# A hybrid decoder trunk on one core: the buffers of the two rings of split weights begin 64 bytes further each

## The chip, the cores and the metric

The kernel runs on 1 core of one Trainium2 chip. Its time is the device time of one execution in microseconds; three executions of the kernel before gave 1941.78, 1944.04 and 1953.4, the median being 1944.04 us.

## The reference

Two layers of a decoder trunk over one sequence of 256 tokens, 1024 channels wide, all in float32. Per layer:

```python
mod = silu(c) @ w_ada[l] + b_ada[l]            # shifts, scales, gates
h = x * (1 + sc1) + sh1
proj = h @ w_in[l]                             # feeds four mixers
y = einsum('bsnc,ncd->bsnd', four_mixers(proj), w_br[l])
mix = (sigmoid(gates) * y).sum(branches) @ w_out[l]
x = layer_norm(alpha * x + g1 * mix)
h = x * (1 + sc2) + sh2
f = swiglu(h)            # layer 0: dense, 2816 wide
f = moe_swiglu(h)        # layer 1: 8 experts of 3584, 2 per token
x = layer_norm(alpha * x + g2 * f)
```

The four mixers are block attention with ALiBi, retention, an SSD scan and stick-breaking attention. Nearly all of the bytes are weights, which are read once.

## The kernel before

Every weight is multiplied as a sum of two parts. A weight tile of 128 partitions by 2048 floats (1 MB) arrives from memory in a tile `raw`. Half of it, 128 by 1024, is then split: ScalarE copies it into a tile `whi` of the type float32r, which keeps its upper bits, and VectorE subtracts that copy from the original and writes the rest into `wlo` (`split_upto`, lines 286 to 310). The activations are split in the same way (hhi and hlo, ohi and olo, ghi and glo, ehi and elo). A product is then three matmuls, high by high, high by low and low by high (`mm3`, lines 380 to 385).

`whi` and `wlo` are two rings of HALVES = 5 tiles, each 4,096 bytes of a partition. `half` (line 339) has the splitting run AHEAD = 3 halves in front of the matmuls that use them. `raw` is a ring of 3 tiles, to which 5 tiles `raw2` come in the second layer's expert part (RAW and RAW2, line 238), so that five of eight places there are raw2. Each `raw` that has been split makes room, and SyncE issues the next transfer in its queue (`emit_dma`, line 240), in an order of weights that is fixed in a list (`build_order`). A few more places for tiles lie in crow, acc, ghi, glo and others that are free at that time (`emit_into`, line 263).

The mixers' projections and the gate and up parts of the dense feed-forward stream the 256 tokens of hhi and hlo through loaded pieces of 128 by 128 of whi and wlo (256 columns each). The experts stream 512 columns of whi or wlo through loaded activations of up to 128 tokens (ghi, glo, ehi, elo).

The pools of tiles lie one behind the other in a partition's memory of 229,376 bytes: constants, `x`, hhi and hlo, the rows (crow and acc among them), then the pool `st` with raw, whi and wlo in the order of their first use, and behind it the tiles of a mixer or of a feed-forward part, which take each other's place. The starts, in bytes of a partition:

| tiles | start | remainder by 512 |
|---|---|---|
| hhi, hlo | 33,216 and 41,408 | 448 |
| crow, acc | 49,600 and 57,792 | 448 |
| raw, 3 of 8,192 | 74,240 | 0 |
| whi, 5 of 4,096 | 98,816 | 0 |
| wlo, 5 of 4,096 | 119,296 | 0 |
| first tile behind the rings | 139,776 | 0 |
| raw2, 5 of 8,192 | 147,968 | 0 |
| ghi, glo, 3 each of 4,096 | 188,928 and 201,216 | 0 |
| ohi, olo, 3 each of 4,096 | 195,232 and 207,520 | 160 |
| end of the highest tile | 228,464 | |

Of the kernel before, what the change touches and what calls it, by code (L numbers as in the profile page):

```python
# [9 lines left out]
F32 = mybir.dt.float32  # L10
F32R = mybir.dt.float32r
# [7 lines left out]
P = 128  # L19
# [125 lines left out]
def trunk(ctx: ExitStack, tc: tile.TileContext, I, out, dbg=None):  # L145
    nc = tc.nc
    pe, act, dve, pool = nc.tensor, nc.scalar, nc.vector, nc.gpsimd
# [6 lines left out]
    st = ctx.enter_context(tc.tile_pool(name="st", bufs=1))  # L154
# [83 lines left out]
    RAW, RAW2, HALVES, AHEAD = 3, 5, 5, 3  # L238
# [34 lines left out]
    def pop_raw(i):  # L273
        raws.pop(i)
        again.pop(i, emit_dma)()

    def raw_upto(i):

        while state["raw"] < i:
            n = state["raw"]  # L280
            if order[n][1] is not None:
                order[n][1](raws[n])
                pop_raw(n)
            state["raw"] += 1

    def split_upto(q):
        while state["half"] <= min(q, 2 * len(hls) - 1):
            q0 = state["half"]
            i, h = hls[q0 // 2], q0 % 2
            raw_upto(i)  # L290
            hi = st.tile([P, 1024], F32R, name="whi", bufs=HALVES)
            lo = st.tile([P, 1024], F32R, name="wlo", bufs=HALVES)
            if isinstance(raws[i], tuple):
                m = len(raws[i]) // 2
                src = raws[i][h * m:(h + 1) * m]
            else:
                n = 512 if q0 in (0, 2 * len(hls) - 1) else 1024
                src = [raws[i][:, c:c + n] for c in range(h * 1024, (h + 1) * 1024, n)]
            n = 1024 // len(src)
            for j, raw in enumerate(src):  # L300
                c = slice(j * n, (j + 1) * n)
                act.activation(hi[:, c], raw, AF.Copy)  # L302
                while later:
                    later.pop()()
                dve.tensor_sub(lo[:, c], raw, hi[:, c].bitcast(F32))  # L305
                late_lo()
            parts[q0] = (hi, lo)
            if h == 1:
                pop_raw(i)
            state["half"] += 1  # L310
# [28 lines left out]
    def half(fs):  # L339

        q = state["done"]
        split_upto(q)
        flush()
        split_upto(q + AHEAD)
        for f in fs(*parts.pop(q)):
            f()
        state["done"] += 1
        step()
        if q - state["mix"] in EXTRA[state["mix"] > 0]:
            step()  # L350

    def by_token(fs, end):

        q = state["done"]
        for i in range(4):
            split_upto(q + i)
            flush()
            split_upto(min(q + i + AHEAD, q + HALVES - 1))
            for f in fs(0, i, *parts[q + i]):
                f()  # L360
            step()
        end(0)
        for i, h in ((0, 1), (0, 2), (1, 1), (1, 2), (2, 1), (3, 1), (2, 2), (3, 2)):
            for f in fs(h, i, *parts[q + i]):
                f()
            if h == 2:
                parts.pop(q + i)
                state["done"] += 1
                step()
            elif i == 3:  # L370
                end(1)
        end(2)
# [88 lines left out]
    def late_lo():  # L461
        while los:
            dve.tensor_sub(*los.pop())
# [1136 lines left out]
```

## Time and profile before

| what | us |
|---|---|
| median of three executions | 1944.04 |
| lowest and highest | 1941.78 and 1953.4 |
| the profiled execution | 1946.45 |
| its span, first to last instruction | 1944.6 |
| TensorE busy | 1884.3 |
| VectorE busy | 1623.0 |
| ScalarE busy | 1200.6 |
| GpSimd busy | 187.8 |

The profile is that of one execution. Matmuls overlap, so their durations add up to more than the time they take; how fast TensorE goes is read from the distance of two starts. The granted clock of TensorE is given as a share of 2.4 GHz. The first layer's mixer lasts to about 380 us, its dense feed-forward to about 565 us, the second layer's mixer to about 940 us, and the experts take the rest.

### The profile page before, as it was taken

Reading aid. Unit: us, or ns where it says so; the run is one execution under the profiler, and the core shown is the slowest. Engines: PE = TensorE matmul, PEld = TensorE weight load, DVE = VectorE, ACT = ScalarE, POOL = GpSimd, SP = SyncE. Lnnn points to the kernel's source line nnn. Section 1 sums busy time; section 2 is a strip of 40 time slices with the busy share of each in tenths; the row PEclk is TensorE's granted clock in tenths of the full one; section 3 lists DMA queues with packets and bytes.
Section 4 is the critical chain, followed back from the end, with each engine's and each line's share of the span. In section 5 each row is a group of like instructions: output and inputs, shape, how many; then the busy total and the mean of one; then the engine's idle time right before and its main releaser. Section 6 shows DMA issues by size and latency. Waiting matters only on the chain. (4 is left out here: it accounts for less than half of the span.)

```text
span 1944.6 us, 29158 instructions
## 1 busy us (share of the span) xinstructions
PE 1884.3 (97%) x11276; PEld 1642.2 (84%) x11276; DVE 1623.0 (83%) x2017; ACT 1200.6 (62%) x1526; POOL 187.8 (10%) x178
## 2 busy tenths in 40 slices
PE   6999999999999999999999999999999999999997
PEld 5888989899989889999888888888888888888885
DVE  7776876888767687767898999999999899999987
ACT  4546544544445456344677777777777777777774
POOL 0023332110011142320000000000000000000000
PEclk9999999999999999999999999999999999999999
DMA  9565666377744456655899899998999999999992
GB/s 346 189 246 212 232 227 228 133 282 290 283 142 174 173 197 232 237 195 218 325 385 329 323 367 366 360 378 323 362 374 360 372 337 350 376 346 378 361 366 105
DMA packets 84340, 558.14 MB, mean 287 GB/s; under 512 B 9697, under 2 KB 9953, under 8 KB 22242
## 3 DMA queue, kind: packets, MB, share of 16 engines
q1 hardware_dynamic: 82226, 550.30, 75.8%
q0 software_dynamic: 1824, 5.78, 0.9%
q8 instruction: 90, 1.47, 0.3%
q14 instruction: 56, 0.46, 0.1%
q10 hardware_dynamic: 144, 0.11, 0.0%
HBM read 555.12 MB, written 1.05 MB: 286 GB/s over the span
## 5 line engine op out<-in xcount | busy, mean ns | idle before, releaser
L305 DVE TENSOR_TENSOR wlo<-raw,whi 128x1024 fp32r<-128x1024 f32 (+1 forms) x880 | 1048.9, 1232 | 202.9 <-ACT whi L302 201.2
L302 ACT ACTIVATE whi<-raw 128x1024 fp32r<-128x1024 f32 (+1 forms) x880 | 881.0, 1050 | 143.2 <-DMA raw<-in_win_dram 29.3
L382 PE MATMUL mm<-hhi,whi 128*128 128x256 f32 x1376 | 393.9, 286 | 19.2 <-ACT whi L302 15.5
L384 PE MATMUL mm<-hhi,wlo 128*128 128x256 f32 x1376 | 387.5, 282 | 8.2 <-DVE wlo L305 8.2
L383 PE MATMUL mm<-hlo,whi 128*128 128x256 f32 x1376 | 387.3, 281 | 0.5 <-DVE hlo L580 0.3
L382 PE MATMUL mm<-whi,ghi 128*128 128x512 f32 x896 | 350.0, 391 | 0.0
L384 PE MATMUL mm<-whi,glo 128*128 128x512 f32 x896 | 349.2, 390 | 0.0
L383 PE MATMUL mm<-wlo,ghi 128*128 128x512 f32 x896 | 348.8, 389 | 0.0
L382 PEld LDWEIGHTS mm<-hhi,whi 128*128 128x128 f32 x1376 | 264.5, 192 | 28.1 <-ACT whi L302 17.6
L384 PEld LDWEIGHTS mm<-hhi,wlo 128*128 128x128 f32 x1376 | 264.0, 192 | 9.0 <-DVE wlo L305 9.0
L383 PEld LDWEIGHTS mm<-hlo,whi 128*128 128x128 f32 x1376 | 264.1, 192 | 1.6 <-DVE hlo L580 1.0
L384 PEld LDWEIGHTS mm<-whi,glo 128*128 128x128 f32 x896 | 168.2, 188 | 35.8
L383 PEld LDWEIGHTS mm<-wlo,ghi 128*128 128x128 f32 x896 | 168.3, 188 | 34.9
L382 PEld LDWEIGHTS mm<-whi,ghi 128*128 128x128 f32 x896 | 168.2, 188 | 33.9
L382 PE MATMUL mx<-whi,ehi 128*128 128x512 f32 x448 | 179.9, 402 | 0.0
L384 PE MATMUL mx<-whi,elo 128*128 128x512 f32 x448 | 175.1, 391 | 0.0
L383 PE MATMUL mx<-wlo,ehi 128*128 128x512 f32 x448 | 174.6, 390 | 0.0
L391 ACT ACTIVATE ehi<-mx 128x512 fp32r<-128x512 f32 x56 | 33.6, 600 | 114.8 <-PE mx L1390 114.8
L384 PEld LDWEIGHTS mx<-whi,elo 128*128 128x128 f32 x448 | 84.1, 188 | 18.2
L383 PEld LDWEIGHTS mx<-wlo,ehi 128*128 128x128 f32 x448 | 84.4, 188 | 15.7
L382 PEld LDWEIGHTS mx<-whi,ehi 128*128 128x128 f32 x448 | 84.2, 188 | 15.8
L438 DVE SCALAR_TENSOR_TENSOR raw<-raw,crow 128x1024 f32<-128x1024 f32 x64 | 78.2, 1259 | 8.6 <-ACT crow L423 6.9
(355 smaller groups left out, 2436.6 us busy)
## 6 DMA issues: line engine op xcount, KB each, us to landing
raw<-in_egu_dram SPq DMA_DIRECT2D x205, 1024.0 KB, 7.0
raw<-in_edn_dram SPq DMA_DIRECT2D x96, 1024.0 KB, 6.9
raw<-in_win_dram SPq DMA_DIRECT2D x79, 1024.0 KB, 4.9
raw<-in_adaT_dram SPq DMA_DIRECT2D x31, 1024.0 KB, 5.1
raw<-in_fgu_dram SPq DMA_DIRECT2D x22, 1024.0 KB, 4.9
raw<-in_adaR_dram SPq DMA_DIRECT2D x16, 1024.0 KB, 4.9
raw<-in_wbr_dram SPq DMA_DIRECT2D x16, 1024.0 KB, 4.9
raw<-in_fdn_dram SPq DMA_DIRECT2D x11, 1024.0 KB, 5.3
```

Source lines behind the costliest of these rows:

```text
L302: act.activation(hi[:, c], raw, AF.Copy)
L305: dve.tensor_sub(lo[:, c], raw, hi[:, c].bitcast(F32))
L382: pe.matmul(ps, a[0], b[0], start=start, stop=False, **kw)
L383: pe.matmul(ps, a[0], b[1], start=False, stop=False, **kw)
L384: pe.matmul(ps, a[1], b[0], start=False, stop=stop, **kw)
L391: act.activation(hi, src, AF.Copy)
L438: dve.scalar_tensor_tensor(r, r, 1.0, crow, op0=ALU.mult, op1=ALU.mult, accum_out=m[:, i, j:j + 1])
```

## The change

Each tile of the two rings is allocated 1040 floats wide and used in its first 1024. Between the two rings a tile of 48 floats is allocated once, and GpSimd fills it with zeros; nothing reads it. All else is as before.

```diff
             raw_upto(i)
-            hi = st.tile([P, 1024], F32R, name="whi", bufs=HALVES)
-            lo = st.tile([P, 1024], F32R, name="wlo", bufs=HALVES)
+
+            hi = st.tile([P, 1040], F32R, name="whi", bufs=HALVES)[:, 0:1024]
+            if q0 == 0:
+                pool.memset(st.tile([P, 48], F32, name="off", bufs=1), 0.0)
+            lo = st.tile([P, 1040], F32R, name="wlo", bufs=HALVES)[:, 0:1024]
             if isinstance(raws[i], tuple):
```

## Rows read from the trace of the kernel before

**Rows 1.** The page, busy us (share of the span) and instructions of each engine

```profile
PE 1884.3 (97%) x11276; PEld 1642.2 (84%) x11276; DVE 1623.0 (83%) x2017; ACT 1200.6 (62%) x1526; POOL 187.8 (10%) x178
```

**Rows 2.** Busy time by stretch; columns in its second line

```profile
core 0: us, PE busy (x) PEld busy (x) DVE busy (x) ACT busy (x) POOL busy (x), PEclk, DMA share, GB/s
400.00:500.00 100.00, 100.00 (x884) 100.00 (x884) 79.45 (x109) 49.20 (x76) 0.00 (x0) 1.00 0.80 301
...
1200.00:1300.00 100.00, 99.76 (x449) 81.73 (x448) 91.68 (x89) 74.50 (x84) 0.00 (x0) 1.00 0.95 364
...
1700.00:1800.00 100.00, 99.76 (x449) 81.66 (x449) 91.91 (x89) 76.22 (x85) 0.00 (x0) 1.00 0.96 362
```

**Rows 3.** Timeline of PE, dense feed-forward; start us, duration us, instruction

```profile
419.76 0.28 PE L382 MATMUL mm<-hhi,whi 128*128 128x256 f32 x1
...
421.91 0.28 PE L383 MATMUL mm<-hlo,whi 128*128 128x256 f32 x1
```

**Rows 4.** Timeline of PE, the first layer's mixer

```profile
329.80 0.28 PE L383 MATMUL mm<-hlo,whi 128*128 128x256 f32 x1
...
331.92 0.28 PE L383 MATMUL mm<-hlo,whi 128*128 128x256 f32 x1
```

**Rows 5.** Timeline of PE, experts

```profile
1539.77 0.39 PE L383 MATMUL mm<-wlo,ghi 128*128 128x512 f32 x1
...
1542.94 0.39 PE L382 MATMUL mm<-whi,ghi 128*128 128x512 f32 x1
```

**Rows 6.** Groups of VectorE, 1000 to 1900 us; busy us, mean ns, idle before

```profile
L305 DVE TENSOR_TENSOR wlo<-raw,whi 128x1024 fp32r<-128x1024 f32 x561 | 654.3, 1219 | 54.8 <-ACT whi L302 53.8 <-DMA raw<-in_egu_dram 0.8 <-DMA acc<-in_egu_dram 0.3
...
L305 DVE TENSOR_TENSOR wlo<-acc,whi 128x1024 fp32r<-128x1024 f32 x26 | 31.7, 1218 | 0.0
L305 DVE TENSOR_TENSOR wlo<-crow,whi 128x1024 fp32r<-128x1024 f32 x26 | 31.6, 1217 | 0.3 <-ACT whi L302 0.3
```

**Rows 7.** Groups of ScalarE, 1000 to 1900 us

```profile
L302 ACT ACTIVATE whi<-raw 128x1024 fp32r<-128x1024 f32 x561 | 556.9, 1052 | 27.1 <-DVE eg L1409 11.0 <-PE mx L384 6.4 <-PE mm L384 5.6
...
L302 ACT ACTIVATE whi<-crow 128x1024 fp32r<-128x1024 f32 x26 | 27.3, 1051 | 0.1
L302 ACT ACTIVATE whi<-acc 128x1024 fp32r<-128x1024 f32 x26 | 27.2, 1046 | 0.3 <-DMA raw<-in_egu_dram 0.3
```

**Rows 8.** Timeline of PE, a branch's projection in the first layer's mixer

```profile
345.96 0.28 PE L382 MATMUL mm<-ohi,whi 128*128 128x256 f32 x1
...
347.38 0.28 PE L382 MATMUL mm<-ohi,whi 128*128 128x256 f32 x1
```

**Rows 9.** DMA issues; out<-in, queue, count, KB each, median us to landing

```profile
raw<-in_egu_dram SPq DMA_DIRECT2D x205, 1024.0 KB, 7.0
...
crow<-in_egu_dram SPq DMA_DIRECT2D x14, 512.0 KB, 7.2
acc<-in_egu_dram SPq DMA_DIRECT2D x14, 512.0 KB, 6.7
...
ghi<-in_egu_dram SPq DMA_DIRECT2D x3, 512.0 KB, 10.6
glo<-in_egu_dram SPq DMA_DIRECT2D x3, 512.0 KB, 6.6
```

**Rows 10.** Timeline of POOL from the start; in brackets the idle time before

```profile
0.82 0.11 POOL L408 MEMSET nhalf<- 128x16 f32 x1
0.86 0.14 POOL L697 MEMSET pad<- 128x6 f32 x2
58.23 0.10 POOL L697 MEMSET pad<- 128x6 f32 x1 [57.23 <-DVE a L708]
```

**Rows 11.** Groups of PE, whole span, those with whi at high by high

```profile
L382 PE MATMUL mm<-hhi,whi 128*128 128x256 f32 x1376 | 393.9, 286 | 19.2 <-ACT whi L302 15.5 <-DVE hhi L577 3.7
...
L382 PE MATMUL mm<-whi,ghi 128*128 128x512 f32 x896 | 350.0, 391 | 0.0
...
L382 PE MATMUL mx<-whi,ehi 128*128 128x512 f32 x448 | 179.9, 402 | 0.0
...
L382 PE MATMUL mm<-ohi,whi 128*128 128x256 f32 x256 | 73.9, 289 | 2.1 <-ACT ohi L391 2.1
```

## The prediction

> **What bounds the kernel now.** I read the page's busy times first, then the busy time by stage, then the matmuls one after the other, and at last the writers of the two rings. TensorE is busy in 97% of the span and VectorE in 83% [rows 1]. By stage, TensorE has no idle time that counts either in the dense feed-forward stretch (400 to 500 us) or among the experts; among the experts VectorE stands at 92% and the DMA engines at 0.95 to 0.96, so two others are close behind [rows 2]. The clock granted to TensorE is 1.00 of full speed, the 2.4 GHz level, in these stretches. So the time is the number of matmuls times their spacing, plus the restarts in the mixers. The change adds no matmul and takes none away; it could only act through the spacing, through the durations of the instructions that fill the rings, or through a transfer.
>
> The spacing is the difference of two starts, since the durations of matmuls overlap. In the feed-forward the 256-column matmuls follow each other every (421.91 - 419.76)/19 = 0.1132 us, with 20 starts in the stretch [rows 3]. Elsewhere the same kind of matmul, with the same three operands hhi, hlo and whi or wlo at the same addresses, goes at (331.92 - 329.80)/18 = 0.1178 us [rows 4]. So there are two paces, and the addresses of the rings don't choose between them. Among the experts the 512-column matmuls come every (1542.94 - 1539.77)/14 = 0.2264 us [rows 5], twice the faster pace.
>
> **The change, part by part.** A tile of a ring takes 4,160 bytes of a partition in place of 4,096. With `raw` first in its pool, whi then starts at 98,816 + 4,160 i in place of 98,816 + 4,096 i. Its five tiles add 5 x 64 = 320 bytes and `off` adds 192, together 512, so wlo starts at 119,808 + 4,160 i in place of 119,296 + 4,096 i. What lies behind the rings (all of the mixers' and feed-forward's tiles, raw2 among them) moves by 320 + 192 + 320 = 832 bytes; the highest end goes from 228,464 to 229,296, and it must stay under 229,376, which it does by 80. In what follows an address's residue is its remainder by 512. Before: raw, whi, wlo, raw2, ghi, glo have 0, hhi, hlo, crow and acc 448, ohi and olo 160. After: whi and wlo have 0, 64, 128, 192, 256 by tile, raw keeps 0, hhi, hlo, crow and acc keep 448, raw2, ghi and glo get 320, ohi and olo 480. No two operands that differed by a whole number of 64 bytes stop doing so, and no start moves by part of 64 bytes.
>
> *Filling wlo (VectorE).* Today raw and whi, the two inputs, have the same residue, and 561 subtractions take 1219 ns on the mean. With crow in raw's place, residue 448 beside whi's 0, 26 of them take 1217 ns, and with acc 26 take 1218 ns [rows 6]. So the distance between the two inputs is worth at most 2 ns of 1219. Applied to all of these 561 that is 1 us of VectorE in 900, and VectorE isn't the engine that binds. I take 0 us.
>
> *Filling whi (ScalarE).* From raw to whi at equal residues 1052 ns, from crow 1051, from acc 1046 [rows 7]. At most 6 ns each, on an engine with a quarter of its time idle among the experts [rows 2]. 0 us.
>
> *Reading the rings (TensorE).* The mixers and the gate and up projections of the dense feed-forward stream hhi (residue 448) and load whi (0); the experts stream whi (0) and load ghi (0). Both give the same nanoseconds per column, 0.1132/256 and 0.2264/512, both 0.442 [rows 3, 5]. The pair of different residues is no faster than the pair of equal ones, and while both go on, VectorE, ScalarE and the transfers write other tiles of the same rings and rings beside them. The nearest row for a bad place is ohi, residue 160, a streamed operand that starts at an odd multiple of 32 bytes: (347.38 - 345.96)/12 = 0.1183 us, against 0.1178 for hhi at the slower pace [rows 8, 4]. I take 0 us, since hhi's row is the nearest one: its start is, like all of the new ones, a multiple of 64. The ends are kept for the rivals.
>
> *Transfers.* raw doesn't move; raw2, five of the eight places in the experts' ring, moves. Half tiles of 512 KB land in crow and acc, 192 bytes above a multiple of 256, in 7.2 and 6.7 us, and in ghi and glo, at a multiple of 256, in 10.6 and 6.6 us [rows 9]; the order says nothing for an even start. I take 0 us. The Trainium skill, in "DMA: Bandwidth & Descriptors", section "How a descriptor splits into AXI transactions", says that a descriptor which doesn't begin at a multiple of 256 bytes has a partly used first transaction; by it, as an estimate, an 8,192-byte row of raw2, now 64 bytes above such a multiple, needs 33 transactions where it needed 32. That speaks against the change; even so five eighths of 3% on a share of 0.96 leaves it under 1, and the sum would still be 0 us.
>
> *The added memset (GpSimd).* One instruction for 48 elements, ahead of the memsets of `pad`. A memset of 16 elements took 0.11 us, and GpSimd then stands still for 57.23 us [rows 10]. It waits for nothing, nothing reads its tile, and what is queued behind it on its engine is those two memsets, whose tile ScalarE fills only when the first projection is done. 0.1 us, hidden; with no cover it would be 0.1 us.
>
> Sum: 0 us on the profiled execution's own 1946.45 us (span 1944.6 and 1.85 around it). That run lies 2.4 us above the median of the three, 1944.04, so I forecast the median again, **1944 us**. The two paces of the 256-column matmuls are left as an unknown inside this: a stretch like that of rows 4 may begin or end elsewhere, and some 60 us at 0.1178 in place of 0.1132 is 2.4 us; two or three of these either way is 7 us.
>
> **Rivals.**
>
> *Faster: equal residues are what slows TensorE.* If a column took one cycle at the granted 2.4 GHz, 256 columns would be 106.7 ns and 512 would be 213.3, so 6.5 and 13.1 ns would be lost in each matmul. If that loss came from the rings' lined-up starts, four of five tiles would be free of it. There are 3 x (1376 + 256) = 4896 matmuls of 256 columns and 3 x (896 + 448) = 4032 of 512 [rows 11]: 0.8 x 4896 x 6.5 ns = 25 us and 0.8 x 4032 x 13.1 ns = 42 us, the latter as much as the DMA share of 0.95 to 0.96 leaves room for [rows 2]. That is 67 us, **1877 us**. Against it: the loss is the same per column at residues 448 with 0 and 0 with 0 [rows 3, 5]. 4%.
>
> *Slower: TensorE reads some of the new places at the slow pace.* If a start away from residue 0 or 448 costs what lies between the two paces, 4.6 ns for 256 columns and by estimate twice that for 512, then four fifths of the matmuls pay: 0.8 x (4896 x 4.6 + 4032 x 9.2) ns = 48 us, **1992 us**. It decides as soon as one tile in five pays it (12 us). For it: ohi at another residue is a little above hhi [rows 8]. Against it: 0.5 ns, not 4.6, and its start is an odd multiple of 32 bytes. 4%.
>
> *Slower: transfers into raw2 get longer and the DMA engines bind.* With a share of 0.96 and five eighths of the tiles affected, TensorE waits from 0.04/(0.96 x 0.625) = 6.7% longer transfers on. At 10% the share would be 1.02 and the 900 us of experts between 1000 and 1900 us would grow by 18 us, **1962 us**. Against it: the landings into crow and acc [rows 9]. 3%. The rule of the Trainium skill on descriptors would do this if its extra transaction weighed more than its share of the 33.
>
> *The change doesn't do what it says.* If the allocator rounded tiles to larger steps, the rings would not fit under the limit above, with 80 bytes left; and if it left them where they are, the time would be the same, 1944 us. 1%, counted with no change.
>
> **Numbers.** Forecast 88%. One per cent (19 us) is about what a measurement of this kernel can tell from no change; by that bound the chance of no change is 0.88 and 1%, a little less for mishaps on both sides that I haven't named: 0.87. Faster 0.06, slower 0.07. The range holds the forecast's own spread: 7 us for the paces and the spread of the three runs (1941.78 to 1953.4), whose median moves less than its ends: 1938 to 1952 us. The rivals, 12% in all, are left outside.
>
> **What would show it.** In the changed kernel's profile: starts still 0.1132 us apart in the feed-forward and 0.2264 among the experts; wlo from raw at 1217 to 1220 ns and whi from raw at 1050 to 1053; TensorE at 97%; the median landing of raw from the experts' weights near 7.0 us. A spacing under 0.112 or over 0.119 us in the feed-forward, or a TensorE share among the experts under 0.99 with waits of ScalarE for raw, would make the prediction wrong.

## The result: 1.1% slower, and the profile after

The changed kernel takes 1967.09 us (median of four executions, 1965.06 to 1971.62) against 1942.91 of the kernel before (1940.64 to 1953.4) on the same chip: a ratio of 1.0109, with a 95% interval of 1.0082 to 1.0136. The forecast was 1944 us with a range up to 1952, so the result lies 15 us above the range. The profiled execution took 1968.43 us, 22 us more than before's 1946.45; its span is 1966.7.

The page's busy line, which answers to [rows 1]:

```profile
PE 1909.5 (97%) x11276; PEld 1652.8 (84%) x11276; DVE 1624.8 (83%) x2017; ACT 1200.6 (61%) x1526; POOL 187.6 (10%) x179
```

TensorE is busy 25.2 us longer (1909.5 - 1884.3) with the same 11276 matmuls. VectorE grew by 1.8 us, ScalarE and GpSimd not at all. So the time did not go into waits: TensorE is full and its matmuls take longer on the mean.

Busy time by stretch of the changed kernel, columns as in [rows 2]; the last two stretches are wider ones, for counts:

```profile
400.00:500.00 100.00, 100.00 (x860) 100.00 (x859) 78.80 (x108) 49.12 (x74) 0.00 (x0) 1.00 0.78 293
1200.00:1300.00 100.00, 99.77 (x441) 80.65 (x440) 91.01 (x88) 74.78 (x83) 0.00 (x0) 1.00 0.95 359
396.00:510.00 114.00, 114.00 (x975) 114.00 (x975) 90.36 (x122) 56.31 (x83) 0.94 (x2) 1.00 0.77 289
1000.00:1900.00 900.00, 898.39 (x4041) 729.90 (x4040) 817.91 (x829) 668.72 (x754) 1.06 (x2) 1.00 0.94 353
```

The same two wide stretches of the kernel before:

```profile
396.00:510.00 114.00, 114.00 (x1007) 114.00 (x1007) 91.28 (x123) 58.06 (x86) 0.00 (x0) 1.00 0.80 298
1000.00:1900.00 900.00, 898.34 (x4096) 739.32 (x4095) 828.62 (x839) 679.47 (x766) 1.07 (x2) 1.00 0.95 358
```

At an unchanged busy time and a granted clock of 1.00 TensorE gets through fewer matmuls: 975 in place of 1007 in 114 us, 4041 in place of 4096 in 900 us. VectorE, ScalarE and the DMA share went down with it.

The matmuls one after the other, in the dense feed-forward: two halves of the ring of the changed kernel, the first one loaded from a whi at remainder 192 by 512, the second from remainder 0; the last two rows are among the experts, in a half whose whi is at remainder 256:

```profile
400.38 0.28 PE L386 MATMUL mm<-hlo,whi 128*128 128x256 f32 x1
...
402.78 0.28 PE L385 MATMUL mm<-hhi,whi 128*128 128x256 f32 x1
...
409.15 0.28 PE L385 MATMUL mm<-hhi,whi 128*128 128x256 f32 x1
...
410.40 0.28 PE L387 MATMUL mm<-hhi,wlo 128*128 128x256 f32 x1
...
1209.40 0.40 PE L385 MATMUL mx<-whi,ehi 128*128 128x512 f32 x1
...
1210.80 0.39 PE L385 MATMUL mx<-whi,ehi 128*128 128x512 f32 x1
```

From the first to the second row are 20 distances, (402.78 - 400.38)/20 = 0.120 us; from the third to the fourth 11, (410.40 - 409.15)/11 = 0.1136. The tile at remainder 0, where all of them were before, keeps the pace of [rows 3]; the tile at 192 doesn't. Among the experts there are six distances of (1210.80 - 1209.40)/6 = 0.2333 us, against 0.2264 of [rows 5]. Over the whole stretch from 396 to 510 us the mean spacing by tile of the ring (the whi and the wlo of a half have the same remainder) is 113.4 ns at remainder 0, 118.4 at 64, 117.7 at 128, 120.0 at 192 and 113.3 at 256: each tile of the ring has a pace of its own.

VectorE, then ScalarE, 1000 to 1900 us, the rows that answer to the first ones of [rows 6] and [rows 7]:

```profile
L308 DVE TENSOR_TENSOR wlo<-raw,whi 128x1024 fp32r<-128x1024 f32 x550 | 641.8, 1220 | 58.1 <-ACT whi L305 57.0 <-DMA raw<-in_egu_dram 0.8 <-DMA acc<-in_egu_dram 0.3
...
L305 ACT ACTIVATE whi<-raw 128x1024 fp32r<-128x1024 f32 x548 | 544.1, 1051 | 31.3 <-PE mx L387 17.8 <-PE mm L387 13.5
```

The DMA issues that answer to [rows 9]:

```profile
raw<-in_egu_dram SPq DMA_DIRECT2D x205, 1024.0 KB, 7.1
...
crow<-in_egu_dram SPq DMA_DIRECT2D x14, 512.0 KB, 7.4
acc<-in_egu_dram SPq DMA_DIRECT2D x14, 512.0 KB, 7.1
...
ghi<-in_egu_dram SPq DMA_DIRECT2D x3, 512.0 KB, 10.9
glo<-in_egu_dram SPq DMA_DIRECT2D x3, 512.0 KB, 7.3
```

The splitting takes 1220 and 1051 ns as before. Ahead of its copies from raw, ScalarE now waits 17.8 + 13.5 = 31.3 us for TensorE to free ring tiles, where the two rows for TensorE were 6.4 + 5.6 = 12.0 [rows 7]; VectorE's wait for raw is the same 0.8. The transfers shown land 0.1 to 0.7 us later.

To size it I took from both traces the distance from each of the 10,026 matmuls of `mm3` to the next one and averaged those without a break, that is without a wait of TensorE between the two (under 130 ns for 256 columns, 250 ns for 512):

| streamed and loaded | columns | before ns | after ns | sum us |
|---|---|---|---|---|
| hhi, hlo with whi, wlo | 256 | 114.76 | 117.13 | +9.2 |
| whi, wlo with ghi, glo | 512 | 227.40 | 231.35 | +10.6 |
| whi, wlo with ehi, elo | 512 | 228.11 | 231.46 | +4.3 |
| all others | | | | +1.8 |

By these means the matmuls that follow each other without a break take 26 us longer in all; the last matmul starts 21.9 us later, which leaves some 4 us less for the breaks. Of the 21.9 us, 8.0 had been lost when the first expert began, and 14 among the experts.

### The profile page after: what moved, and what is told of

The parts are those of the page before. It is cut to its first block, busy times and chain, and to the rows that moved or that the text cites. A ratio compares the mean times of both kernels' runs of the same rounds, so it can differ in the third digit from the quotient of the medians.

```text
span 1966.7 us, 29159 instructions
## 1 busy us (share of the span) xinstructions
PE 1909.5 (97%) x11276; PEld 1652.8 (84%) x11276; DVE 1624.8 (83%) x2017; ACT 1200.6 (61%) x1526; POOL 187.6 (10%) x179
```

## Experiments

**The theory.** While TensorE streams one operand it loads the next one (PEld is busy in all of the 100 us of the feed-forward in [rows 2]). The theory, worked out from the result, is that its pace depends on the distance between the two starts, d = (start of the loaded operand - start of the streamed one), taken by remainder of 256 bytes. Before, every expert matmul had d = 0 (whi 0, ghi 0), and every projection that streams hhi or hlo d = 64 (whi 0, hhi 448, so -448). After, by tile of the ring, the experts have 64, 0, 192, 128, 64 (ghi now at 320), and the projections 64, 128, 192, 0, 64. The rivals: what counts is where the operand stands by itself; the strides or the distance of whi from wlo, which meet while ScalarE and VectorE write; or the transfers into raw2, which moved as well.

**Pairs by themselves (m1_pairs).** The matmuls alone, without the trunk: one streamed tile, loaded tiles that begin 32 bytes further each.

```diff
+    W = sp.tile([P, 1152], F32R, name="mov")
+    S = [sp.tile([P, 136], F32R, name=f"s{32 * i}") for i in range(NS)]
...
+        for k in range(REP):
+            pe.matmul(ps[:, 0:cols], s[:, 0:128], W[:, off:off + cols], start=True, stop=True)
```

> Only matmuls, on numbers from x: 24 matmuls in a row for each of 20 loaded operands whose starts lie 0, 32, 64 ... 608 bytes above a multiple of 512, with a streamed operand that starts at such a multiple, first 512 and then 256 columns; then the streamed operand moves by 64 bytes at a time; then 256 columns again with a break ahead of each group; then beside busy ScalarE and VectorE. The trunk is left out, and the output is x. Theory of the pair (TensorE streams one operand and at the same time loads the next one, and goes slower at some distances between their two starts, by the remainder by 256): the spacing of the starts changes from group to group, from 0.2267 us to about 0.231 to 0.236 for 512 columns and from 0.1133 to 0.118 to 0.120 for 256, the same pattern comes back after 256 bytes, it is there with the other engines idle, and it is the same beside busy engines. Rival, that other engines or transfers which write the rings slow TensorE: all groups at 0.2267 and 0.1133 as long as nothing else runs, slower ones only in the last part.

Measured, mean distance of two starts in groups of 24 without the first four (ns):

| d, bytes | 0 | 32 | 64 | 96 | 128 | 160 | 192 | 224 |
|---|---|---|---|---|---|---|---|---|
| 512 columns | 226.6 | 233.4 | 233.5 | 234.3 | 233.6 | 233.6 | 228.9 | 233.2 |
| 256 columns | 119.7 | 118.3 | 117.8 | 117.3 | 118.5 | 120.1 | 117.7 | 117.8 |

The pattern repeats from d = 256 on. Where the streamed operand is moved instead, it comes back but for two things: with 512 columns the first of two groups at d = 192 took 233.3 ns, the second one 228.7, and the two at d = 128 took 232.5 and 232.6. So what counts is in the main the distance and not a place, and what ran before has some part. With 512 columns d = 0 is the best distance and 64 costs 6.9 ns. With 256 columns d = 0 is nearly the worst. The 113.3 ns that were expected for 256 columns didn't come in groups that followed each other; after a break, d = 64 went at 113.4 in three of three groups, and so both paces of [rows 3, 4] appear at one and the same d.

**The tail alone (e1_tail832).** The rings stand as before; all that lies behind them moves by 832 bytes, as in the changed kernel. Now d = 64 for every expert matmul; the projections keep 64.

```diff
             lo = st.tile([P, 1024], F32R, name="wlo", bufs=HALVES)
+            if q0 == 0:
+                pool.memset(st.tile([P, 208], F32, name="off", bufs=1), 0.0)
```

> The rings stay as they were before; only what lies behind them moves by 832 bytes, as in the changed kernel. Theory of the pair: among the experts whi and wlo (remainder 0) are streamed against ghi, glo, ehi and elo at remainder 320, so that the 512-column spacing goes from 0.2267 to between 0.231 and 0.233 us and the experts get 17 to 26 us longer; the mixers and the gate and up projections of the dense feed-forward keep their pace within 2 us. 1960 to 1970 us in all. Rival, transfers into raw2 (now 64 bytes above a multiple of 256): the same sum is possible, but with waits of ScalarE for raw and TensorE's spacing unchanged at 0.2267. Rival, the rings' tiles at different places to each other and to raw: 1943 us, nothing moves.

Measured: 1971.53 us against 1945.32, a ratio of 1.0137 (1.0116 to 1.0158), a little above the 1960 to 1970 expected. The kernel with two old rings is as slow as the changed one, so neither the 64 bytes between the tiles nor the distance of the two rings is needed. TensorE among the experts:

```profile
1539.73 0.39 PE L384 MATMUL mm<-whi,ghi 128*128 128x512 f32 x1
...
1543.00 0.39 PE L386 MATMUL mm<-whi,glo 128*128 128x512 f32 x1
```

These are fourteen distances of 0.2336 us, the 233.5 ns of d = 64 in the pairs; the expectation had stopped at 0.233. By stretch:

```profile
396.00:510.00 114.00, 114.00 (x1006) 114.00 (x1005) 91.90 (x124) 58.07 (x86) 0.25 (x1) 1.00 0.80 298
1000.00:1900.00 900.00, 898.44 (x4012) 721.65 (x4011) 810.91 (x822) 663.50 (x749) 1.06 (x2) 1.00 0.94 351
```

The feed-forward keeps its count (1006, before 1007); the experts lose 84 matmuls in 900 us.

**Rings and tail together (e2_all832).** The same 832 bytes ahead of the rings: whi, wlo and ghi move alike, so the experts keep d = 0, and the projections get 128. raw2 stands at remainder 320, as in the changed kernel.

```diff
             raw_upto(i)
+            if q0 == 0:
+                pool.memset(st.tile([P, 208], F32, name="off", bufs=1), 0.0)
             hi = st.tile([P, 1024], F32R, name="whi", bufs=HALVES)
```

> The 832 bytes are put ahead of the rings, so that the rings and all behind them move together; the rings are packed as before. Theory of the pair: among the experts the distance is 0 as before, spacing 0.2267, no loss there, though raw2 lies where it does in the changed kernel; but hhi and hlo stay, so that the 256-column matmuls of mixers and dense feed-forward now have whi at remainder 320 against 448, and go at 0.118 to 0.120 in place of 0.1133 to 0.1178: 10 to 20 us, all before 946 us, 1953 to 1963 in all. Rival, transfers into raw2: experts 14 us longer as in the changed kernel. Rival, the rings' tiles at different places to each other: 1943 us.

Measured: 1959.06 us, ratio 1.0067 (1.0051 to 1.0083). By stretch:

```profile
396.00:510.00 114.00, 114.00 (x955) 114.00 (x955) 88.41 (x120) 55.26 (x82) 1.22 (x2) 0.99 0.77 284
1000.00:1900.00 900.00, 898.41 (x4102) 739.84 (x4101) 830.51 (x842) 678.34 (x765) 1.07 (x2) 1.00 0.95 359
```

Now the feed-forward is slow (955 matmuls, before 1007; the granted clock of 0.99 is a small part of that, since halves in this stretch have a spacing of 118.5 to 118.8 ns) and the experts are as fast as before (4102, before 4096), with raw2 and both operands of the experts at another place than before. That takes out the transfers into raw2 and the place of an operand by itself.

**The tail by 256 bytes (e3_tail256).** As e1_tail832, with 64 floats in place of 208: ghi moves, d stays 0.

```diff
-                pool.memset(st.tile([P, 208], F32, name="off", bufs=1), 0.0)
+                pool.memset(st.tile([P, 64], F32, name="off", bufs=1), 0.0)
```

> The rings stay as before; what lies behind them moves by 256 bytes. Theory of the pair with a period of 256: nothing changes, 1943 us within 5, spacing among the experts 0.2267. The same theory with a period of 512 or more: the experts go at 0.230 or slower and the sum is 1955 or more. Rival, raw2's place by multiples of 256: 1943 us too.

Measured: 1947.35 us, ratio 1.0009 (0.9994 to 1.0023): no difference that can be told. So it isn't the move of the tail but its remainder by 256. The spacing among the experts is 227.66 ns on the mean, before 227.63. Its profiled execution, with a span of 1950.0 us, shows something else in the feed-forward:

```profile
419.84 0.28 PE L386 MATMUL mm<-hhi,wlo 128*128 128x256 f32 x1
...
420.90 0.28 PE L386 MATMUL mm<-hhi,wlo 128*128 128x256 f32 x1
```

Nine distances of 0.1178 us where before had 0.1132 at the same d = 64 [rows 3].

**Pairs again, with longer groups (m2_pairs).** Groups of 48 with a name for each loaded tile (at64b begins 64 bytes behind the streamed operand, by remainder of 512), bfloat16 as well, and groups that were to run beside a busy ScalarE and VectorE.

```diff
-REP = 24
+REP = 48
+STEPS = [32 * i for i in range(16)]
...
+    # no break: what goes ahead of 64
+    for d in (0, 32, 96, 128, 160, 192, 224):
+        group(S[d], 256, 24)
+        group(S[64], 256)
```

> Only matmuls again, in groups of 48, each group with a loaded operand of its own name that says how many bytes its start lies above a multiple of 512 (the streamed one lies at such a multiple); the trunk is left out and the output is x. Theory of the pair, with the values of the first series of matmuls: 512 columns take 0.2266 us at 0 and 256 bytes, 0.2335 at 64, 0.2336 at 128, 0.229 at 192, 0.233 to 0.234 at odd multiples of 32; 256 columns 0.1197 at 0, 0.1178 at 64, 0.1185 at 128, 0.1178 at 192 without a break, and 0.1134 at 64 after a break. If the loading of the next operand is what disturbs, then with loads at 0, 0, 64, 64 in turn a 512-column matmul is slow when the next load is at 64, whatever it multiplies itself; if its own loaded operand is what counts, it is slow when that is at 64. bfloat16, half the bytes for each column: no expectation from the theory but that the loss is smaller. Rival, other engines: the last four groups, beside ScalarE and VectorE, slower than the same groups at the start.

The timeline of PE, each row a group; from a row's start to that of the row right behind it are 48 distances:

```profile
30.57 11.36 PE L50 MATMUL mm<-mov,at64b 128*128 128x512 f32 x48
41.77 11.40 PE L50 MATMUL mm<-mov,at96b 128*128 128x512 f32 x48
...
97.56 11.05 PE L50 MATMUL mm<-mov,at256b 128*128 128x512 f32 x48
108.45 11.35 PE L50 MATMUL mm<-mov,at288b 128*128 128x512 f32 x48
119.64 11.36 PE L50 MATMUL mm<-mov,at320b 128*128 128x512 f32 x48
...
198.06 5.82 PE L50 MATMUL mm<-mov,at64b 128*128 128x256 f32 x48
203.71 5.79 PE L50 MATMUL mm<-mov,at96b 128*128 128x256 f32 x48
...
290.35 5.72 PE L50 MATMUL mm<-mov,at64b 128*128 128x256 f32 x48 [0.43 <-ACT at64b L60]
...
336.85 5.61 PE L50 MATMUL mm<-mov,at64b 128*128 128x256 f32 x48
342.29 3.00 PE L50 MATMUL mm<-mov,at32b 128*128 128x256 f32 x24
...
375.52 2.88 PE L50 MATMUL mm<-mov,at192b 128*128 128x256 f32 x24
378.24 5.61 PE L50 MATMUL mm<-mov,at64b 128*128 128x256 f32 x48
...
403.07 10.53 PE L79 MATMUL mm<-movh,at0h 128*128 128x512 bf16 x48
413.44 10.52 PE L79 MATMUL mm<-movh,at32h 128*128 128x512 bf16 x48
...
539.50 11.36 PE L50 MATMUL mm<-mov,at64b 128*128 128x512 f32 x48
550.70 11.32 PE L50 MATMUL mm<-mov,at128b 128*128 128x512 f32 x48
```

At 64 bytes a matmul takes (41.77 - 30.57)/48 = 0.2333 us, at 256, which is d = 0, (108.45 - 97.56)/48 = 0.2269, and the group at 320, the remainder of ghi after the change, has a duration of 11.36 as at 64. At 128 the first series had 233.6 ns; the groups of 48 took 232.5.

VectorE had nothing to wait for and did its work at the start, up to 52 us, so that it was idle beside the last groups, where ScalarE alone was busy; in the first series of matmuls VectorE was done at 56 us in the same way, and the groups of 256 columns at its end had neither engine beside them. Three groups at d = 64 still give the answer, columns as in [rows 2]:

```profile
30.57:41.77 11.20, 11.20 (x49) 9.02 (x48) 10.93 (x9) 0.00 (x0) 0.00 (x0) 1.00 0.00 0
119.64:130.84 11.20, 11.20 (x49) 9.02 (x48) 0.00 (x0) 0.00 (x0) 0.00 (x0) 1.00 0.00 0
539.50:550.70 11.20, 11.20 (x50) 9.02 (x48) 0.00 (x0) 10.88 (x11) 0.00 (x0) 1.00 0.00 0
```

A group of 48 takes 11.20 us beside VectorE, beside nobody and beside ScalarE, (550.70 - 539.50)/48 = 0.2333 in the last one: the writes of either engine have no part in it. Both at once were not tried.

In bfloat16 all eight starts give (413.44 - 403.07)/48 = 0.2160, so of these two types only float32r depends on d. With 256 columns at 64 bytes there are two paces, (203.71 - 198.06)/48 = 0.1177 early and (342.29 - 336.85)/48 = 0.1133 late. The late groups have no break ahead of them, and they went so whatever d the group ahead had (all seven took 5.60 to 5.63 us). d = 192 has the two paces as well: 0.1177 early, and late, between two fast groups at 64, (378.24 - 375.52)/24 = 0.1133. Within a group the pace stays; what changed it between the early and the late groups isn't shown.

A test in which d changed after each second matmul gave 225 to 241 ns, and with 0 and 64 the mean was 231 to 233 in each of the four positions. So whether a matmul's own operand or the next one's counts it doesn't tell.

**The changed kernel with a tail at 768 (e4_stag768).** The rings as in the change, the tile between them 32 floats rather than 48. raw2 and ghi return to a multiple of 256, and the distances of the experts become 0, 192, 128, 64, 0 for whi and 64, 0, 192, 128, 64 for wlo, the projections' 64, 128, 192, 0, 64 and 0, 64, 128, 192, 0.

```diff
-                pool.memset(st.tile([P, 48], F32, name="off", bufs=1), 0.0)
+                pool.memset(st.tile([P, 32], F32, name="off", bufs=1), 0.0)
```

> The changed kernel with the tile between the rings 64 bytes smaller, so that what lies behind the rings is moved by 768 bytes, three times 256, and raw2, ghi and glo are again at a multiple of 256; the rings' tiles stay 64 bytes further each. Theory of the pair: the distances of whi run through 0, 192, 128, 64, 0 and those of wlo through 64, 0, 192, 128, 64 over the five tiles, which by the first series of matmuls is 0.2305 us on the mean, 3.9 ns above 0.2267; among the experts 16 us more, and about 10 in the mixers and the dense feed-forward as in the changed kernel: 1965 to 1974 us. Rival, raw2's place: 14 of the 24 us come back, 1953 to 1957.

Measured: 1969.11 us, ratio 1.0114 (1.0094 to 1.0135). By stretch:

```profile
1000.00:1900.00 900.00, 898.42 (x4051) 731.37 (x4050) 821.28 (x834) 670.00 (x755) 1.06 (x2) 1.00 0.94 354
```

With raw2 back at an even start the experts are hardly better (4051, after 4041), since three tiles of whi and four of wlo still have another d than 0. From the pairs, with whi streamed twice as often as wlo, they would come at (2 x 229.8 + 231.2)/3 = 230.3 ns; measured are 230.70. That the mean fits doesn't show that each tile behaves as its pair does by itself: in this run, where d changes from one matmul to the next, the experts' matmuls grouped by their own d took 230.8 ns at 0, 229.8 at 64, 230.9 at 128 and 231.5 at 192.

**ohi moved to a better distance (e5_ohi32).** Here the rule is tried the other way round, on the kernel before: 32 bytes ahead of ohi and olo, once a layer, so that the branches' projections get d = 64 in place of 96.

```diff
+    if not state.get(("off", l)):
+        state["off", l] = pool.memset(mp.tile([P, 8], F32, name="off"), 0.0) or True
```

> The kernel before, with 32 bytes put ahead of ohi and olo, so that whi lies 64 bytes above them by the remainder by 256, as it does above hhi. Theory of the pair: the 768 matmuls that stream ohi or olo go from about 0.118 us to between 0.1134 and 0.1178, 0 to 4 us; if the slow pace of hhi, which often follows them, starts less often too, up to 8 us: 1937 to 1945 us, at most just measurable. Rival, that the pair explains the rings alone: 1945 us, ohi's spacing unchanged.

TensorE in a branch's projection, the stretch of [rows 8]:

```profile
345.94 0.28 PE L382 MATMUL mm<-ohi,whi 128*128 128x256 f32 x1
...
347.30 0.28 PE L382 MATMUL mm<-ohi,whi 128*128 128x256 f32 x1
```

These are twelve distances of 0.1133 us in place of 0.1183; on the mean of all of them it is 114.59 in place of 117.82 ns. The slow pace of hhi did not become rarer (115.63 ns on the mean, before 114.76). Measured in all: 1942.76 us, ratio 0.9989 (0.9977 to 1.0001). 3 x 256 matmuls by 3.2 ns are 2.5 us, and an improvement of that size isn't told apart from none. It has the lowest ratio of all versions tried, and is no proven gain.

**All profiled runs together.** Mean distance in ns without breaks, and what these means give with the 3 x 1376 = 4128 projections by hhi and hlo, the 4032 expert matmuls and the 768 of ohi [rows 11], beside the span:

| kernel | hhi, hlo | experts | ohi | worked out, us | span against 1944.6 |
|---|---|---|---|---|---|
| before | 114.76 | 227.63 | 117.82 | 0 | 0 |
| after | 117.13 | 231.38 | 118.17 | +25.2 | +22.1 |
| e1_tail832 | 114.70 | 233.33 | 118.27 | +23.1 | +22.4 |
| e2_all832 | 118.71 | 227.43 | 117.63 | +15.4 | +11.5 |
| e3_tail256 | 115.83 | 227.66 | 117.96 | +4.6 | +5.4 |
| e4_stag768 | 117.76 | 230.70 | 118.04 | +24.9 | +25.6 |
| e5_ohi32 | 115.63 | 227.65 | 114.59 | +1.2 | -1.1 |

The worked-out sums leave out the breaks and the other kinds of matmul; they lie within 4 us of the spans.

## Why the prediction was wrong

*Reading the rings (TensorE)* is the step that failed: "I take 0 us", and before it "there are two paces, and the addresses of the rings don't choose between them". It was worth 22 to 25 us. Two errors are in it. It compared hhi (448) with whi (0) and whi (0) with ghi (0), found 0.442 ns per column in both, and took them for a bad and a good place that give the same. By distance they are d = 64 and d = 0, and each is as good as any for its own width: 0.1134 us for 256 columns, 0.2267 for 512. Two optima looked like indifference. And it then called hhi "the nearest one: its start is, like all of the new ones, a multiple of 64", as if an operand's own start counted. ohi, which it set aside, was a hint: at d = 96 it took 117.82 ns on the mean (the pairs give 117.3), and none of its distances is under 115, where hhi has 113.3 in the feed-forward. Another hint was in the trace and not looked at: the 512-column matmuls that stream whi and wlo through a loaded hhi or hlo, d = 192, took 229.15 ns on the mean, against 227.63 among the experts; the pairs give 228.9 for that distance. The pairs also foretell what the change makes of ohi, d = 32, 96, 160, 224 and 32 by tile: (118.3 + 117.3 + 120.1 + 117.8 + 118.3)/5 = 118.4, measured 118.17.

That the two paces of [rows 3, 4] have the same addresses was right; that the addresses therefore have no say was not. At d = 64 either pace can be taken, and beside that there is a dependence on d. In the changed kernel's feed-forward the two can be told apart, since each half of the ring has one d: 113.3 and 113.4 ns at 64, 118.4 at 128, 117.7 at 192 and 120.0 at 0, each within 0.3 of a value of the pairs.

*The rival "TensorE reads some of the new places at the slow pace"* is the nearest to what happened, at half its price: 24 us in place of 48. Its condition was another one, a start away from remainder 0 or 448; in the changed kernel a whi at 256 kept 113.3 ns under hhi, and in e2_all832 whi, wlo, ghi and glo all stand at 320 and the experts lost nothing. It had 4.6 ns for 256 columns on four tiles of five, measured were 2.4 on the mean of all (114.76 to 117.13); for 512 columns 9.2 on four of five, which is 7.4 on the mean, measured 3.75 (227.63 to 231.38). From the pairs the experts come out at (233.5 + 226.6 + 228.9 + 233.6 + 233.5)/5 = 231.2 ns. Its 4% was low for a rival that had a row of the trace for it and only the size of that row against it. The range left out all rivals and so the result too.

*The rival "equal residues are what slows TensorE"* had the sign wrong for 512 columns, where d = 0 is the best. With 256 columns d = 0 is indeed slow (120.0 ns), but no projection by hhi stood there before; the change put one tile of five there.

*What would show it:* of the signs named, the one for a wrong forecast came, a spacing over 0.119 us in the feed-forward (0.120), and so did a spacing other than 0.2264 among the experts; TensorE's share of 97% said nothing, since a full engine stays full when it gets slower.

*Filling wlo, filling whi, the memset:* right, 1220 and 1051 ns, and GpSimd's busy time is unchanged with one instruction more.

*Transfers:* right as far as the waits go. raw lands in 7.1 us in place of 7.0, VectorE waits for it no longer than before (0.8 us), and ScalarE's 31.3 us ahead of its copies from raw are all for TensorE. The rival on transfers into raw2 fell with e2_all832, which has raw2 at the same uneven start and lost nothing among the experts. The rule on descriptors in the Trainium skill, "DMA: Bandwidth & Descriptors", section "How a descriptor splits into AXI transactions", adds one transaction to 32 by estimate. The section tells it of the bytes that a transaction reads, and raw2 is the side that is written; no run here shows a cost of it.

The Trainium skill, "TensorE: Matmul & The Clock Gate", section "Step-by-step: what each phase is for", says that the array has two read ports, so that loading the next weights takes no read bandwidth from the matmul in progress. In bfloat16 the pairs agree, 0.2160 us at all starts. In float32r a matmul that has the next load beside it takes 226.6 or 233.5 ns by how the two operands lie, which that sentence doesn't lead one to expect, and the measurement decides. No run leaves the loading out, so that it is the loading that costs the 6.9 ns is argued and not shown.

**What stays open.** Why a distance of 64 bytes should cost what it does, inside TensorE or in the memory it reads, no run shows. Nor do they show which of two neighbouring operands it is that counts. In the changed kernel the experts' matmuls grouped by their own d are closer together (0: 228.9, 64: 232.5, 128: 231.3, 192: 231.6 ns) than the pairs by themselves. All operands that the experts load there have the same remainder, so it makes no difference whether the own or the next loaded one is counted. Each tile serves six matmuls, and a pace that takes some of them to settle would give such means; that is only argued. And what picks 0.1132 or 0.1178 us at d = 64, or at 192, is not known; the feed-forward had the fast pace in the profiled run of before and the slow one in those of e3_tail256 and e5_ohi32, some 4 us, which may be a part of the spread between executions of one kernel.

## What to carry to other kernels

Where TensorE is full, work out for each kind of matmul the distance of its two operands by remainder, and look at the spacing per kind before moving anything: a move of one buffer changes the pair with everything that stays. Two rows that agree show that a quantity doesn't matter only if they differ in that quantity and are alike in the rest; here they differed in the width as well, and each was at a good distance for its own width. A padding tile of 256 bytes that shifts the rest made no difference here (e3_tail256), one of 832 cost 1.4% (e1_tail832).

## What the runs showed of the hardware that was not expected

- The spacing of float32r matmuls goes by the distance of the loaded from the streamed operand, with a period of 256 bytes. With 512 columns it was 226.6 ns at 0, 228.9 at 192 (in one group 233.3) and 232.3 to 234.3 elsewhere; with 256 columns 113.3 or 117.7 at 64 and at 192, and 116.7 to 120.1 elsewhere.
- The best distance isn't the same for both widths: 0 is the best for 512 columns and, with 160, the worst for 256.
- At a distance of 64 bytes 256-column matmuls have two lasting paces, 4% apart, at the same operands and a granted clock of 1.00.
- In bfloat16 512 columns took 216 ns at each of eight starts.
